# Seven-product projection: all sums on VectorE, and v units of four token blocks

## The chip, the cores and the metric

One core of a Trainium2 chip runs the whole program. The metric is device microseconds (us) of one execution; a profiled execution also gives its span, from the first to the last instruction. The engines are TensorE (PE; PEld is its weight load), VectorE (DVE), ScalarE (ACT), GpSimd (POOL) and SyncE (SP), whose queue issues most DMAs.

## What is computed

A two-layer trunk on 2048 prompt frames and 64 further frames (2112 columns, T), width 1024, four heads:

```
for each layer i:                       # 0: differential attention, 1: stick-breaking attention
    h = rmsnorm(x, norm_w[i])
    q, k, v, g = split(h @ w_in[i], 4)  # 1024 x 4096
    x = x + (mixer_i(q, k, v, past) * silu(g)) @ w_out[i]
y = rmsnorm(x, final_norm_w)            # returned with the new k and v rows of both layers
```

All matrices are fp32. A matmul is made of three: each operand is split into hi (a rounded copy, by ACT) and lo (the rest, x - hi, by DVE or POOL), and lo*hi, hi*lo and hi*hi are summed in PSUM.

## The kernel before, in words

Layer 0 runs `p_phase` (projection), `a_phase` (attention) and `o_phase` (output); layer 1 runs `p_strassen`, `a_phase` and `o_phase`. The change lies in layer 1's projection, `p_strassen` (L349), in `stage_steps` (L318), which prepares its input and runs inside layer 0's `o_phase` and inside `p_strassen`, and in the few lines that hand the norm's factors over.

`p_strassen` multiplies 2x2 block matrices with seven products in place of eight. The tokens come in two passes: pass 0 has two blocks of 512 tokens, pass 1 two blocks of 512 + 32. Seven operands of the token side (sums of blocks) lie in DRAM (`xop`); `fill` (L379) loads each in four chunks through three buffers `xraw` (pool `sf`, 3 buffers), and each chunk is split by ACT (L53) and by `split`'s second engine (L54). The seven operands X stand in SBUF for the whole pass, and are refilled for pass 1 product by product during the last unit of pass 0 (L573).

The work is a list of units (L513 to L518). Pass 0: head 0's k, q, gate; four v units; for heads 1 to 3 gate, k, q. Pass 1: four heads' k and q; v, v, s, v, v, s; four gates. A "p" unit (k, q or gate of one head) has seven products of 12 matmuls with 512 columns (pass 0) or 24 with 272 columns (pass 1). A v unit holds two token blocks of 128, seven products of 24 matmuls with 256 columns, one block to a PSUM bank. An s unit is the 64 left-over tokens' v, classically.

For each unit `seven` (L400) loads four weight quarters (two sets for v), forms four sums (L406, L407, L409 on POOL, L411), and `halves` (L387) splits seven operands `wop` (14 for v; ACT L53, then L54). `wop` has five buffers; `more`/`take` (L523, L528) run that far ahead of the products. `other()` (L375) gives the lo of each split in turn to POOL and to DVE.

A unit's seven products go to four PSUM tags of two banks each: a, e, c, d, and again a, c, d, accumulated onto what stands there. Between them ACT copies a or c out (L579, L584, L592) and DVE adds a product to an SBUF tile `e` (L581, L587, L596, L599; ten buffers); L588 is on POOL. Four times a unit `finish` (L439) stores a result: for q, k and v a split into `s` and DMAs, for a gate a silu of L457 ACT, L458 DVE, L459 and L460 ACT, L461 POOL, L462 and L463 DVE. PE may start product 5 only when L579 has read bank a, and product 7 only when L587 has read bank d.

`stage_steps` for pass 1 runs one step after each of units 3 to 6 (the v units of pass 0), L606: eight loads, eight scalings (L334, four of them of 32 columns), four sums (L337, L338; L342 and L343 on POOL), four small stores and seven stores. Unit 7 frees its tiles and loads `xs`.

The order of instructions within each engine's queue is set at build time, by a scheduler that goes by priorities and its own estimate of times, not strictly by program order; each queue then runs in order.

Of the kernel before, what the change touches and what calls it, by code (L numbers as in the profile page):

```python
# [17 lines left out]
P = 128  # L18
# [3 lines left out]
NS = 64  # L22
# [33 lines left out]

def mm3(nc, ps, lh, ll, rh, rl, start, stop):
    nc.tensor.matmul(ps, lh, rl, start=start, stop=False, skip_group_check=True)  # L58
    nc.tensor.matmul(ps, ll, rh, start=False, stop=False, skip_group_check=True)  # L59
    nc.tensor.matmul(ps, lh, rh, start=False, stop=stop, skip_group_check=True)  # L60
# [257 lines left out]
def stage_steps(nc, k, pas, xv, rr, alloc):  # L318

    w, sides = PASSES[pas]
    dst = k.xop[pas]
    for c in range(4):
        b = {}
        for d in range(2):
            for t in range(2):
                b[d, t] = q = alloc()[:, :w]
                for p0, t0, n in sides[t]:  # L330
                    nc.sync.dma_start(out=q[:, p0:p0 + n], in_=xv[:, c + 4 * d, t0:t0 + n])
        for (d, t), q in b.items():
            for (p0, t0, n), r in zip(sides[t], rr[t]):
                nc.vector.scalar_tensor_tensor(q[:, p0:p0 + n], q[:, p0:p0 + n], k.wnm[:, c + 4 * d:c + 4 * d + 1],  # L334
                                               r, ALU.mult, ALU.mult)
# [6 lines left out]
        nc.gpsimd.tensor_tensor(b[0, 1], b[1, 1], b[0, 1], ALU.subtract)  # L342
        nc.gpsimd.tensor_tensor(t4, b[1, 0], t2, ALU.subtract)  # L343
        for i, q in enumerate((b[0, 0], t2, t1, b[0, 1], b[1, 0], b[1, 1], t4)):
            nc.sync.dma_start(out=dst[i, :, c, :w], in_=q)
        yield


def p_strassen(tc, k, layer, xsrc, rb, close):  # L349
# [7 lines left out]
    with ExitStack() as es:  # L357
# [8 lines left out]
        xv = xsrc.rearrange("(c p) t -> p c t", p=P)  # L366
        turn = [0]

# [5 lines left out]

        def other():  # L375
            turn[0] += 1
            return nc.gpsimd if turn[0] % 2 else nc.vector

        def fill(pas, op):  # L379
            w = PASSES[pas][0]  # L380
            X[op] = t = xp.tile([P, 2, 4, PW], F32R, tag=f"x{op}", name="x")
            for c in range(4):
                raw = rp.tile([P, PW], F32, tag="r", name="xraw")[:, :w]
                nc.sync.dma_start(out=raw, in_=k.xop[pas][op, :, c, :w])
                split(nc, t[:, 0, c, :w], t[:, 1, c, :w], raw, other())

        def halves(a):  # L387
            t = wop.tile([P, 2, 512], F32R, tag="w", name="wop")
            split(nc, t[:, 0], t[:, 1], a, other())
            return t  # L390
# [9 lines left out]
        def seven(a11, a12, a21, a22):  # L400

            a11, a21, a22 = raws((a11, a21, a22))
            s1 = wrp.tile([P, 512], F32, tag="w", name="s1")
            s2 = wrp.tile([P, 512], F32, tag="w", name="s2")
            a12, = raws((a12,))
            nc.vector.tensor_tensor(s1, a21, a22, ALU.add)  # L406
            nc.vector.tensor_tensor(s2, s1, a11, ALU.subtract)  # L407
            yield halves(a11)
            nc.gpsimd.tensor_tensor(a21, a11, a21, ALU.subtract)  # L409
            yield halves(s2)  # L410
            nc.vector.tensor_tensor(s2, a12, s2, ALU.subtract)  # L411
# [26 lines left out]

        def finish(u, o, fh, th):  # L439

            w = PASSES[u.pas][0]
            if u.kind == "v":
                hs = slice((u.i + 2 * fh) * HW, (u.i + 2 * fh + 1) * HW)
                t0 = PASSES[u.pas][1][th][0][1] + u.b * 256
# [3 lines left out]
                split(nc, s2[:, 0, :512], s2[:, 1, :512], o[:, :512], other())  # L448
                for i in range(2):
# [5 lines left out]
            if u.s == 3:  # L455
# [13 lines left out]
            s2 = sp.tile([P, 2, PW], F32R, tag="s2", name="s2")  # L469
            split(nc, s2[:, 0, :w], s2[:, 1, :w], o, other())  # L470
            store(lambda t0, n: dst[r0:r0 + P, :, t0:t0 + n], lambda p0, n: s2[:, :, p0:p0 + n].bitcast(F32), th, u.pas)

        def product(u, ps, ws, x, start):
            if u.kind == "v":
                for b in range(2):
                    t = slice((2 * u.b + b) * P, (2 * u.b + b + 1) * P)
                    for c in range(4):
                        ce = slice(c % 2 * HW, c % 2 * HW + HW)
                        mm3(nc, ps[:, b, :HW], x[:, 0, c, t], x[:, 1, c, t], ws[c // 2][:, 0, ce],
                            ws[c // 2][:, 1, ce], start and c == 0, c == 3)  # L480
                return
# [9 lines left out]
        def unit(pas, kind, **kw):  # L491
# [3 lines left out]
            u.__dict__.update(kw)  # L495
            u.n, u.subs = (HW, 2) if kind == "v" else ((512, 1), (272, 2))[pas]
            u.tiles = 1 if kind == "p" else 2
# [59 lines left out]
        for n, u in enumerate(units):  # L557
# [5 lines left out]

            def view(t):
                return t[:, :u.subs * u.n].rearrange("p (b n) -> p b n", b=u.subs)

            def run(op, tag, start):
# [5 lines left out]
                if refill:  # L573
                    fill(1, op)
                return ps[tag][:, :u.subs, :u.n]

            a = run(0, "a", True)
            m = e()
            nc.scalar.activation(view(m), a, AF.Copy)  # L579
            b = run(1, "e", True)  # L580
            nc.vector.tensor_tensor(view(m), view(m), b, ALU.add)  # L581
            c = run(2, "c", True)
            m5 = e()
            nc.scalar.activation(view(m5), c, AF.Copy)  # L584
            d = run(3, "d", True)
            x = e()
            nc.vector.tensor_tensor(view(x), view(m), d, ALU.add)  # L587
            nc.gpsimd.tensor_tensor(view(m5), view(x), view(m5), ALU.add)  # L588
            finish(u, m5, 1, 1)
            a = run(4, "a", False)  # L590
            o = e()
            nc.scalar.activation(view(o), a, AF.Copy)  # L592
            finish(u, o, 0, 0)
            c = run(5, "c", False)
            o = e()
            nc.vector.tensor_tensor(view(o), view(m), c, ALU.add)  # L596
            finish(u, o, 0, 1)
            d = run(6, "d", False)
            nc.vector.tensor_tensor(view(m), view(m), d, ALU.add)  # L599
            finish(u, m, 1, 0)  # L600
            if n == 0:
                stats(nc, k, k.acc, TT[0][1], lambda: bank("a")[:, 0], rb[:, 832:1088], None, e(), e())
                staging = stage_steps(nc, k, 1, xv, ((rb[:, :512], rb[:, 1024:1056]), (rb[:, 512:1024], rb[:, 1056:1088])), e)
            elif n >= 3 and staging is not None:
                if next(staging, 0) == 0:
                    staging = None  # L606
                    close()
                    xs = es.enter_context(pool(tc, f"sv{layer}", side="right")).tile([P, 2, NC, NS], F32R, name="xs")
                    raw = e()[:, :NC * NS].rearrange("p (c t) -> p c t", c=NC)
                    nc.sync.dma_start(out=raw, in_=k.xs)  # L610
                    split(nc, xs[:, 0], xs[:, 1], raw, nc.vector)

# [360 lines left out]
def o_phase(tc, k, layer, resid, rb):  # L973
# [3 lines left out]
    with ExitStack() as es:  # L977
# [39 lines left out]
        for n, ti in enumerate((1, 2, 3, 4, 0) if last else (1, 3, 2, 4, 0)):  # L1017
# [196 lines left out]
```

## Time and profile before

| | us |
|---|---|
| median of 3 runs (3048.54 to 3050.07) | 3049.37 |
| the profiled execution, own time | 3052.32 |
| its span | 3050.3 |
| of that, `p_strassen` (1528 to 2318) | 790 |
| mean granted TensorE clock over the span | 0.97 |

The profile's rows come from the one profiled execution. "Busy" is the time in which an engine has an instruction running; an instruction that stands and waits for something inside itself is busy too. Matmuls overlap one another, so a PE busy all the time is not yet PE at its best. A wait names the instruction that ended it.

### The profile page before, as it was taken

How to read it: one execution, taken by the hardware profiler on the slowest of the kernel's cores; microseconds unless marked ns; L12 is line 12 of the kernel's file. 1: busy time of each engine (PE TensorE's matmuls, PEld its weight loads, DVE VectorE, ACT ScalarE, POOL GpSimd, SP SyncE). 2: the span in 40 equal slices, each digit the busy share in tenths (PEclk: the TensorE clock that was granted, in tenths of full speed). 3: DMA queues.
4: the chain of work that ended last, by engine and by line, in shares of the span. 5: the costliest groups of instructions: out<-in, count | busy, mean ns of one | idle time of the engine just before them, and what ended most of it. 6: DMA issues, size and time to landing. Idle time of an engine off the chain costs nothing. (4 is left out here: it accounts for less than half of the span.)

```text
span 3050.3 us, 46001 instructions
## 1 busy us (share of the span) xinstructions
PE 2850.7 (93%) x16342; PEld 2473.8 (81%) x16342; DVE 2010.3 (66%) x3266; ACT 1420.8 (47%) x2706; POOL 1175.2 (39%) x1053
## 2 busy tenths in 40 slices
PE   8899999999899999999977899799897999999998
PEld 7888998989777777778857777699796778888788
DVE  8754625245688777854558877655886878878454
ACT  5321221212566665643244344444455777776433
POOL 4533333333144343551256755645763000000221
PEclk9999999999999999999988999999997999999999
DMA  5476556463633425155756844655746344433442
GB/s 164 152 204 180 143 156 171 144 162 113 231 133 130 141 95 181 63 169 185 243 183 217 274 145 148 219 191 190 228 131 207 117 150 137 134 125 101 159 148 95
DMA packets 370550, 492.43 MB, mean 161 GB/s; under 512 B 64016, under 2 KB 208656, under 8 KB 370320
## 3 DMA queue, kind: packets, MB, share of 16 engines
q1 hardware_dynamic: 355168, 475.06, 49.0%
q10 hardware_dynamic: 15152, 14.44, 1.4%
q8 instruction: 128, 2.10, 0.3%
q14 instruction: 102, 0.84, 0.1%
HBM read 281.49 MB, written 207.88 MB: 160 GB/s over the span
## 5 line engine op out<-in xcount | busy, mean ns | idle before, releaser
L58 PE MATMUL pj<-x,wop 128*128 128x272 f32 (+1 forms) x1008 | 336.8, 335 | 48.0 <-POOL x L54 19.2
L58 PE MATMUL pj<-hl,whi 128*128 128x512 f32 (+2 forms) x960 | 341.0, 355 | 2.6 <-ACT whi L53 1.9
L59 PE MATMUL pj<-hh,wlo 128*128 128x512 f32 (+2 forms) x960 | 338.8, 353 | 0.1
L60 PE MATMUL pj<-hh,whi 128*128 128x512 f32 (+2 forms) x960 | 338.4, 353 | 0.0
L59 PE MATMUL pj<-x,wop 128*128 128x272 f32 (+1 forms) x1008 | 332.5, 330 | 0.1
L60 PE MATMUL pj<-x,wop 128*128 128x272 f32 (+1 forms) x1008 | 331.8, 330 | 0.0
L58 PE MATMUL s<-k,q 128*128 128x512 f32 (+3 forms) x656 | 268.6, 410 | 33.7 <-POOL k L54 13.5
L58 PE MATMUL o<-wl,v 128*128 128x512 f32 (+4 forms) x688 | 270.1, 393 | 17.4 <-DVE wl L54 9.9
L58 PEld LDWEIGHTS pj<-x,wop 128*128 128x128 f32 x1008 | 193.6, 192 | 80.0 <-POOL x L54 24.0
L54 DVE TENSOR_TENSOR wl<-tp,wh 128x512 fp32r<-128x512 f32 (+5 forms) x344 | 195.2, 575 | 93.3 <-ACT wh L53 92.9
L60 PE MATMUL o<-wh,v 128*128 128x512 f32 (+4 forms) x688 | 249.8, 363 | 0.0
L59 PE MATMUL o<-wh,v 128*128 128x512 f32 (+4 forms) x688 | 249.5, 363 | 0.0
L60 PE MATMUL s<-k,q 128*128 128x512 f32 (+3 forms) x656 | 245.2, 374 | 0.0
L59 PE MATMUL s<-k,q 128*128 128x512 f32 (+3 forms) x656 | 244.8, 373 | 0.0
L53 ACT ACTIVATE s<-o 128x256 fp32r<-128x256 f32 (+2 forms) x212 | 84.1, 404 | 337.9 <-DMA kS<-s 127.4
L58 PE MATMUL ps<-ol,wh 128*128 128x512 f32 (+2 forms) x640 | 227.8, 356 | 6.4 <-DVE ol L54 6.4
L53 ACT ACTIVATE wh<-tp 128x512 fp32r<-128x512 f32 (+5 forms) x344 | 170.8, 508 | 131.1 <-PE tp L776 115.2
L59 PE MATMUL ps<-oh,wl 128*128 128x512 f32 (+2 forms) x640 | 229.6, 359 | 0.0
L60 PE MATMUL ps<-oh,wh 128*128 128x512 f32 (+2 forms) x640 | 227.0, 355 | 0.0
L59 PEld LDWEIGHTS pj<-x,wop 128*128 128x128 f32 x1008 | 194.7, 193 | 15.0 <-DVE wop L54 0.6
L60 PEld LDWEIGHTS pj<-x,wop 128*128 128x128 f32 x1008 | 194.0, 193 | 15.6
L58 PEld LDWEIGHTS pj<-hl,whi 128*128 128x128 f32 x960 | 182.0, 190 | 26.5 <-ACT whi L53 2.1
(231 smaller groups left out, 7887.7 us busy)
## 6 DMA issues: line engine op xcount, KB each, us to landing
wraw<-in_wqkg SPq DMA_DIRECT2D x144, 256.0 KB, 3.9
vS<-s SPq DMA_DIRECT2D x128, 256.0 KB, 3.2
v<-vS SPq DMA_DIRECT2D x64, 512.0 KB, 5.3
q<-qS SPq DMA_DIRECT2D x60, 512.0 KB, 5.2
k<-kS SPq DMA_DIRECT2D x60, 512.0 KB, 7.8
wraw<-in_wv SPq DMA_DIRECT2D x96, 256.0 KB, 3.8
qS<-s SPq DMA_DIRECT2D x128, 128.0 KB, 2.4
kS<-s SPq DMA_DIRECT2D x128, 128.0 KB, 2.4
```

The source lines that it names most:

```text
L53: nc.scalar.activation(hi, x, AF.Copy)
L54: lo_eng.tensor_tensor(lo, x, hi.bitcast(F32), ALU.subtract)
L58: nc.tensor.matmul(ps, lh, rl, start=start, stop=False, skip_group_check=True)
L59: nc.tensor.matmul(ps, ll, rh, start=False, stop=False, skip_group_check=True)
L60: nc.tensor.matmul(ps, lh, rh, start=False, stop=stop, skip_group_check=True)
```

## The change

Within `p_strassen` and `stage_steps` every sum that POOL made goes to DVE: `other()` is gone and all lo parts are DVE's, as are L409, L461, L588, L342 and L343. A v unit takes four token blocks, two to a PSUM bank (the second block's first matmul has no start flag and is pinned behind the first block's matmuls), so there are two v units for four in each pass, and each weight operand is made once for four blocks; each PSUM bank is read by an instruction of its own, into an `e` tile of its own. The stage's steps for pass 1 go from behind units 3 to 6 to behind units 6, 7, 9 and 10 of the new numbering (head 1's k and q, head 2's k and q), its end to behind unit 11 (head 3's gate). The norm's factors lie as 2 x 544 columns, so one scaling of 544 columns takes the place of one of 512 and one of 32; three ACT copies put the left-over columns in place after unit 0.

```
 def mm3(nc, ps, lh, ll, rh, rl, start, stop, pin=None):
+    first = nc.tensor.matmul(ps, lh, rl, ...)
+    if pin is not None: pin(first)
 ...
 # stage_steps
-            for (p0, t0, n), r in zip(sides[t], rr[t]):
-                nc.vector.scalar_tensor_tensor(q[:, p0:p0 + n], ...)
+            nc.vector.scalar_tensor_tensor(q, q, k.wnm[...], rr[t], ALU.mult, ALU.mult)
-        nc.gpsimd.tensor_tensor(b[0, 1], ...)     # and t4
+        nc.vector.tensor_tensor(b[0, 1], ...)     # and t4
 ...
 # fill, halves, finish
-                split(..., other())
+                split(..., nc.vector)
 # seven, finish (gate)
-            nc.gpsimd.tensor_tensor(a21, a11, a21, ALU.subtract)
+            nc.vector.tensor_tensor(a21, a11, a21, ALU.subtract)
-                nc.gpsimd.tensor_tensor(a, a, r, ALU.mult)
+                nc.vector.tensor_tensor(a, a, r, ALU.mult)
 ...
 # product, v
-                for b in range(2):
-                    t = slice((2 * u.b + b) * P, (2 * u.b + b + 1) * P)
+                for b in range(4):
+                    t = slice(b * P, b * P + P)
+                    o = ps[:, b // 2, b % 2 * HW:b % 2 * HW + HW]
                     for c in range(4):
-                        mm3(nc, ps[:, b, :HW], ..., start and c == 0, c == 3)
+                        mm3(nc, o, ..., start and c == 0 and b % 2 == 0, c == 3,
+                            tc.keep_in_program_order if start and c == 0 and b % 2 else None)
 # values
-                for b in range(2):
-                    unit(pas, "v", i=i, b=b)
+                unit(pas, "v", i=i)
 ...
 # a unit: two pieces for v, one for the others
+            if u.kind == "v":
+                cut = [(lambda t, i=i: t[:, i], lambda t: t[:, :512]) for i in range(2)]
-            m = e()
-            nc.scalar.activation(view(m), a, AF.Copy)
+            m = [e() for _ in cut]
+            for (b, v), t in zip(cut, m):
+                nc.scalar.activation(v(t), b(a), AF.Copy)
 ...                                               # likewise for e, c, d, a, c, d
-            nc.gpsimd.tensor_tensor(view(m5), view(x), view(m5), ALU.add)
+                nc.vector.tensor_tensor(v(t5), v(tx), v(t5), ALU.add)
 ...
             if n == 0:
+                r = e()[:, :256]
+                stats(nc, k, k.acc, ..., r, None, e(), e())
+                for c0, c1, r0 in ((0, 192, 864), (192, 224, 512), (224, 256, 1056)):
+                    nc.scalar.activation(rb[:, r0:r0 + c1 - c0], r[:, c0:c1], AF.Copy)
+                staging = stage_steps(nc, k, 1, xv, (rb[:, :PW], rb[:, PW:]), e)
-            elif n >= 3 and staging is not None:
+            elif n in (6, 7, 9, 10):
+                next(staging)
+            elif n == 11:
+                next(staging, None)
+                close()
 ...
```

## Rows read from the trace of the kernel before

**Rows 1.** The page's part 1: busy time, share of the span and number of instructions of each engine.
```profile
PE 2850.7 (93%) x16342; PEld 2473.8 (81%) x16342; DVE 2010.3 (66%) x3266; ACT 1420.8 (47%) x2706; POOL 1175.2 (39%) x1053
```
**Rows 2.** Busy time by stage: layer 1's input side (the end of layer 0's `o_phase`) and `p_strassen`. Columns: stretch, its length, then busy us (and instructions) of each engine, granted clock, DMA share, GB/s.
```profile
1345.00:1528.00 183.00, 176.77 (x925) 153.86 (x923) 96.91 (x137) 51.55 (x97) 45.47 (x36) 0.99 0.66 220
1528.00:2318.00 790.00, 705.39 (x4466) 636.75 (x4466) 557.81 (x598) 362.90 (x640) 493.37 (x328) 0.95 0.58 187
```
**Rows 3.** The same columns for stretches cut at the first matmul of a unit (84 matmuls make a p unit of pass 0, 168 one of pass 1 or a v unit): head 0's k and q; its gate; the four v units; head 1's gate to head 3's k (8 units); head 3's q, and head 0's k and q of pass 1; the next six k and q units; v, v, s, v, v, s; the four gates. Then two single units, pass 1's first v and head 2's k in pass 0, and last a part of the fourth v unit.
```profile
1530.20:1590.80 60.60, 50.27 (x171) 35.54 (x172) 30.08 (x37) 29.14 (x51) 36.13 (x26) 0.85 0.57 182
1590.80:1610.30 19.50, 19.50 (x86) 15.75 (x85) 12.63 (x16) 10.06 (x18) 10.39 (x9) 1.00 0.54 176
1610.30:1729.30 119.00, 95.41 (x674) 92.93 (x673) 106.71 (x114) 51.55 (x90) 86.44 (x55) 0.89 0.78 251
1729.30:1903.40 174.10, 161.57 (x675) 127.04 (x673) 123.35 (x142) 74.52 (x135) 101.33 (x68) 0.97 0.48 161
1903.40:1990.50 87.10, 70.56 (x421) 62.93 (x420) 55.63 (x52) 41.08 (x73) 58.95 (x40) 0.92 0.67 215
1990.50:2117.10 126.60, 126.60 (x1011) 126.60 (x1010) 67.88 (x79) 49.73 (x85) 61.40 (x45) 1.00 0.58 188
2117.10:2228.80 111.70, 95.71 (x770) 91.43 (x769) 87.21 (x84) 60.33 (x107) 85.48 (x55) 1.00 0.74 235
2228.80:2316.80 88.00, 85.75 (x674) 84.50 (x672) 72.41 (x77) 43.64 (x79) 51.25 (x33) 1.00 0.24 75
2117.10:2137.10 20.00, 20.00 (x171) 20.00 (x170) 13.09 (x15) 11.87 (x20) 14.47 (x10) 1.00 0.64 204
1816.30:1844.50 28.20, 22.68 (x85) 17.30 (x84) 22.06 (x23) 13.42 (x25) 18.58 (x12) 0.89 0.31 101
1705.15:1731.30 26.15, 23.38 (x154) 22.49 (x155) 26.07 (x26) 10.97 (x20) 20.94 (x13) 0.87 0.88 290
```
**Rows 4.** PE's waits from 1528 to 2318: who waited for whom, us in total, times, longest.
```profile
PE pj L58 <- DVE wop L54: 26.0, 12, 4.5
PE pj L58 <- POOL x L54: 19.2, 10, 5.9
PE pj L58 <- DVE e L587: 12.3, 7, 4.2
```
**Rows 5.** DVE in order of time, around the last v unit of pass 0: start, us, what.
```profile
1699.64 0.68 DVE L406 TENSOR_TENSOR s<-wraw 128x512 f32<-128x512 f32 x1
1700.24 0.68 DVE L411 TENSOR_TENSOR s<-wraw,s 128x512 f32<-128x512 f32 x1
1700.84 0.67 DVE L599 TENSOR_TENSOR e<-e,pj 128x512 f32<-128x512 f32 x1
...
1711.85 0.71 DVE L337 TENSOR_TENSOR e<-e 128x544 f32<-128x544 f32 x1
1712.49 1.27 DVE L334 SCALAR_TENSOR_TENSOR e<-e,wnm,rb 128x32 f32<-128x32 f32 x1
```
**Rows 6.** POOL in order of time, the same stretch.
```profile
1718.76 1.72 POOL L409 TENSOR_TENSOR wraw<-wraw 128x512 f32<-128x512 f32 x1
1720.45 1.73 POOL L588 TENSOR_TENSOR e<-e 128x512 f32<-128x512 f32 x1
```
**Rows 7.** The instructions of single lines from 1528 to 2318: count, ns min/median/max, first and last start.
```profile
L458 DVE TENSOR_SCALAR e<-e x30: 409/443/1528, 1606.2 to 2319.2; 128x512 f32<-128x512 f32 x16, 128x544 f32<-128x544 f32 x14
L54 DVE TENSOR_TENSOR x<-xraw,x x28: 677/796/1881, 1529.3 to 1973.5; 128x512 fp32r<-128x512 f32 x14, 128x544 fp32r<-128x544 f32 x14
L54 POOL TENSOR_TENSOR x<-xraw,x x28: 1263/1351/1856, 1528.9 to 1975.6; 128x512 fp32r<-128x512 f32 x14, 128x544 fp32r<-128x544 f32 x14
```
**Rows 8.** One chunk's round in the refill, in order of time: SP's issue of the load, ACT's hi, POOL's lo.
```profile
1952.18 2.23 SPq L384 DMA_DIRECT2D xraw<-xop  x3
1954.92 0.66 ACT L53 ACTIVATE x<-xraw 128x544 fp32r<-128x544 f32 x1 [1.74 <-DMA xraw<-xop]
1955.65 1.34 POOL L54 TENSOR_TENSOR x<-xraw,x 128x544 fp32r<-128x544 f32 x1 [2.17 <-ACT x L53]
```
**Rows 9.** Waits of ACT and POOL from 1528 to 2318, as in rows 4.
```profile
POOL wop L54 <- ACT wop L53: 68.9, 42, 4.9
POOL e L461 <- ACT e L460: 51.2, 23, 3.3
POOL s L54 <- ACT s L53: 45.7, 31, 4.0
POOL x L54 <- ACT x L53: 44.7, 17, 12.2
ACT x L53 <- DMA xraw<-xop: 41.9, 29, 5.2
```
**Rows 10.** DVE in order of time in head 2's k unit, behind head 2's gate.
```profile
1834.58 0.68 DVE L462 SCALAR_TENSOR_TENSOR e<-e 128x512 f32<-128x512 f32 x1
1835.18 1.75 DVE L407 TENSOR_TENSOR s<-s,wraw 128x512 f32<-128x512 f32 x1
1836.85 1.75 DVE L463 SCALAR_TENSOR_TENSOR e<-e 128x512 f32<-128x512 f32 x1
1838.52 0.67 DVE L587 TENSOR_TENSOR e<-e,pj 128x512 f32<-128x512 f32 x1
```
**Rows 11.** DMA issues from 1528 to 2318: count, KB each, median us to landing.
```profile
wraw<-in_wv SPq DMA_DIRECT2D x80, 256.0 KB, 3.9
```

More of the change, by code (lines that the diff above doesn't have):

```diff
@@ L54, in split, with mm3 @@
     lo_eng.tensor_tensor(lo, x, hi.bitcast(F32), ALU.subtract)
-def mm3(nc, ps, lh, ll, rh, rl, start, stop):
-    nc.tensor.matmul(ps, lh, rl, start=start, stop=False, skip_group_check=True)
+def mm3(nc, ps, lh, ll, rh, rl, start, stop, pin=None):
+    first = nc.tensor.matmul(ps, lh, rl, start=start, stop=False, skip_group_check=True)
+    if pin is not None:
+        pin(first)
     nc.tensor.matmul(ps, ll, rh, start=False, stop=False, skip_group_check=True)
@@ L332, in stage_steps @@
         for (d, t), q in b.items():
[L333 to L335 removed]
+            nc.vector.scalar_tensor_tensor(q, q, k.wnm[:, c + 4 * d:c + 4 * d + 1], rr[t], ALU.mult, ALU.mult)
         t1, t2, t4 = alloc()[:, :w], alloc()[:, :w], alloc()[:, :w]
@@ L341, in stage_steps @@
                 nc.sync.dma_start(out=k.xs[:, c + 4 * d, 32 * t:32 * t + 32], in_=q[:, 512:544])
-        nc.gpsimd.tensor_tensor(b[0, 1], b[1, 1], b[0, 1], ALU.subtract)
-        nc.gpsimd.tensor_tensor(t4, b[1, 0], t2, ALU.subtract)
+        nc.vector.tensor_tensor(b[0, 1], b[1, 1], b[0, 1], ALU.subtract)
+        nc.vector.tensor_tensor(t4, b[1, 0], t2, ALU.subtract)
         for i, q in enumerate((b[0, 0], t2, t1, b[0, 1], b[1, 0], b[1, 1], t4)):
@@ L366, in p_strassen @@
         xv = xsrc.rearrange("(c p) t -> p c t", p=P)
-        turn = [0]
         def e():
@@ L373, in bank @@
             return psp.tile([P, 2, 512], F32, tag=tag, name="pj")
-        def other():
-            turn[0] += 1
-            return nc.gpsimd if turn[0] % 2 else nc.vector
         def fill(pas, op):
@@ L384, in fill @@
                 nc.sync.dma_start(out=raw, in_=k.xop[pas][op, :, c, :w])
-                split(nc, t[:, 0, c, :w], t[:, 1, c, :w], raw, other())
+                split(nc, t[:, 0, c, :w], t[:, 1, c, :w], raw, nc.vector)
         def halves(a):
             t = wop.tile([P, 2, 512], F32R, tag="w", name="wop")
-            split(nc, t[:, 0], t[:, 1], a, other())
+            split(nc, t[:, 0], t[:, 1], a, nc.vector)
             return t
@@ L437, in store, with finish @@
                 nc.sync.dma_start(out=dst(t0, n), in_=o(p0, n))
-        def finish(u, o, fh, th):
+        def finish(u, o, fh, th, half=0):
             w = PASSES[u.pas][0]
@@ L443, in finish @@
                 hs = slice((u.i + 2 * fh) * HW, (u.i + 2 * fh + 1) * HW)
-                t0 = PASSES[u.pas][1][th][0][1] + u.b * 256
+                t0 = PASSES[u.pas][1][th][0][1] + half * 256
                 nc.sync.dma_start(out=k.v[layer, t0:t0 + 256, hs].rearrange("(b p) e -> p b e", p=P),
@@ L447, in finish @@
                 s2 = sp.tile([P, 2, PW], F32R, tag="s2", name="s2")
-                split(nc, s2[:, 0, :512], s2[:, 1, :512], o[:, :512], other())
+                split(nc, s2[:, 0, :512], s2[:, 1, :512], o[:, :512], nc.vector)
                 for i in range(2):
@@ L469, in finish @@
             s2 = sp.tile([P, 2, PW], F32R, tag="s2", name="s2")
-            split(nc, s2[:, 0, :w], s2[:, 1, :w], o, other())
+            split(nc, s2[:, 0, :w], s2[:, 1, :w], o, nc.vector)
             store(lambda t0, n: dst[r0:r0 + P, :, t0:t0 + n], lambda p0, n: s2[:, :, p0:p0 + n].bitcast(F32), th, u.pas)
@@ L474, in product @@
             if u.kind == "v":
-                for b in range(2):
-                    t = slice((2 * u.b + b) * P, (2 * u.b + b + 1) * P)
+                for b in range(4):
+                    t = slice(b * P, b * P + P)
+                    o = ps[:, b // 2, b % 2 * HW:b % 2 * HW + HW]
                     for c in range(4):
                         ce = slice(c % 2 * HW, c % 2 * HW + HW)
-                        mm3(nc, ps[:, b, :HW], x[:, 0, c, t], x[:, 1, c, t], ws[c // 2][:, 0, ce],
-                            ws[c // 2][:, 1, ce], start and c == 0, c == 3)
+                        mm3(nc, o, x[:, 0, c, t], x[:, 1, c, t], ws[c // 2][:, 0, ce],
+                            ws[c // 2][:, 1, ce], start and c == 0 and b % 2 == 0, c == 3,
+                            tc.keep_in_program_order if start and c == 0 and b % 2 else None)
                 return
@@ L495, in unit @@
             u.__dict__.update(kw)
-            u.n, u.subs = (HW, 2) if kind == "v" else ((512, 1), (272, 2))[pas]
+            u.n, u.subs = (512, 2) if kind == "v" else ((512, 1), (272, 2))[pas]
             u.tiles = 1 if kind == "p" else 2
@@ L562, in p_strassen @@
             ps = {}
-            def view(t):
-                return t[:, :u.subs * u.n].rearrange("p (b n) -> p b n", b=u.subs)
+            if u.kind == "v":
+                cut = [(lambda t, i=i: t[:, i], lambda t: t[:, :512]) for i in range(2)]
+            else:
+                cut = [(lambda t: t[:, :u.subs, :u.n],
+                        lambda t: t[:, :u.subs * u.n].rearrange("p (b n) -> p b n", b=u.subs))]
             def run(op, tag, start):
@@ L574, in run @@
                     fill(1, op)
-                return ps[tag][:, :u.subs, :u.n]
+                return ps[tag]
             a = run(0, "a", True)
-            m = e()
-            nc.scalar.activation(view(m), a, AF.Copy)
-            b = run(1, "e", True)
-            nc.vector.tensor_tensor(view(m), view(m), b, ALU.add)
+            m = [e() for _ in cut]
+            for (b, v), t in zip(cut, m):
+                nc.scalar.activation(v(t), b(a), AF.Copy)
+            f = run(1, "e", True)
@@ L582, in p_strassen @@
+            for (b, v), t in zip(cut, m):
+                nc.vector.tensor_tensor(v(t), v(t), b(f), ALU.add)
             c = run(2, "c", True)
-            m5 = e()
-            nc.scalar.activation(view(m5), c, AF.Copy)
+            m5 = [e() for _ in cut]
+            for (b, v), t in zip(cut, m5):
+                nc.scalar.activation(v(t), b(c), AF.Copy)
             d = run(3, "d", True)
-            x = e()
-            nc.vector.tensor_tensor(view(x), view(m), d, ALU.add)
-            nc.gpsimd.tensor_tensor(view(m5), view(x), view(m5), ALU.add)
@@ L589, in p_strassen @@
-            finish(u, m5, 1, 1)
+            x = [e() for _ in cut]
+            for (b, v), t, tx, t5 in zip(cut, m, x, m5):
+                nc.vector.tensor_tensor(v(tx), v(t), b(d), ALU.add)
+            for i, ((b, v), tx, t5) in enumerate(zip(cut, x, m5)):
+                nc.vector.tensor_tensor(v(t5), v(tx), v(t5), ALU.add)
+                finish(u, t5, 1, 1, i)
             a = run(4, "a", False)
-            o = e()
-            nc.scalar.activation(view(o), a, AF.Copy)
-            finish(u, o, 0, 0)
+            for i, (b, v) in enumerate(cut):
+                o = e()
+                nc.scalar.activation(v(o), b(a), AF.Copy)
+                finish(u, o, 0, 0, i)
@@ L594, in p_strassen @@
             c = run(5, "c", False)
-            o = e()
-            nc.vector.tensor_tensor(view(o), view(m), c, ALU.add)
-            finish(u, o, 0, 1)
+            for i, ((b, v), t) in enumerate(zip(cut, m)):
+                o = e()
+                nc.vector.tensor_tensor(v(o), v(t), b(c), ALU.add)
+                finish(u, o, 0, 1, i)
             d = run(6, "d", False)
-            nc.vector.tensor_tensor(view(m), view(m), d, ALU.add)
-            finish(u, m, 1, 0)
+            for i, ((b, v), t) in enumerate(zip(cut, m)):
+                nc.vector.tensor_tensor(v(t), v(t), b(d), ALU.add)
+                finish(u, t, 1, 0, i)
@@ L601, in p_strassen @@
             if n == 0:
-                stats(nc, k, k.acc, TT[0][1], lambda: bank("a")[:, 0], rb[:, 832:1088], None, e(), e())
-                staging = stage_steps(nc, k, 1, xv, ((rb[:, :512], rb[:, 1024:1056]), (rb[:, 512:1024], rb[:, 1056:1088])), e)
-            elif n >= 3 and staging is not None:
[L605 to L611, printed above, removed]
+                r = e()[:, :256]
@@ new lines, in p_strassen @@
+                stats(nc, k, k.acc, TT[0][1], lambda: bank("a")[:, 0], r, None, e(), e())
+                for c0, c1, r0 in ((0, 192, 864), (192, 224, 512), (224, 256, 1056)):
[6 more added lines that the diff above has]
+                close()
+                xs = es.enter_context(pool(tc, f"sv{layer}", side="right")).tile([P, 2, NC, NS], F32R, name="xs")
+                raw = e()[:, :NC * NS].rearrange("p (c t) -> p c t", c=NC)
+                nc.sync.dma_start(out=raw, in_=k.xs)
+                split(nc, xs[:, 0], xs[:, 1], raw, nc.vector)
@@ L993, in o_phase @@
             ra = es.enter_context(pool(tc, f"ora{layer}")).tile([P, 1024], F32, name="ra")
-            rt = {1: ra[:, :512], 3: ra[:, 512:], 2: rb[:, :512], 4: rb[:, 512:832]}
+            rt = {1: ra[:, :512], 3: ra[:, 512:], 2: rb[:, :512], 4: rb[:, PW:PW + 320]}
         psp = es.enter_context(pool(tc, f"ops{layer}", 6, space=PSUM))
@@ L1060, in o_phase @@
             if ti == 3 and not last:
-                staging = stage_steps(nc, k, 0, yo, ((rt[1],), (rt[3],)),
+                staging = stage_steps(nc, k, 0, yo, (rt[1], rt[3]),
                                       lambda: stp.tile([P, 512], F32, tag="st", name="st"))
```

## Prediction

> **What bounds the kernel now.** I read the page's part 1 first [rows 1]: PE is busy 93% of the span, DVE 66%, POOL 39%. On that alone a change of DVE and POOL would be worth nothing. But the share is a mean over stages, so next comes the busy time by stage [rows 2]. Of `p_strassen`'s 790 us PE is busy 705 (85 idle), its clock is below full (0.95), and POOL is busier (493) than anywhere else. PE's waits in that stage name who ends the idle time [rows 4]: the lo parts of the weights, of the token operands X, and L587, DVE's read of bank d. PE waits for DVE and POOL, not for memory.
>
> The stage has to be cut by unit, since its parts have different limits [rows 3]. Some stretches have a PE that never stops, and these give a floor for each kind of unit: a p unit of pass 0 takes 19.5 us (the first gate), a v unit of two blocks 20.0, a p unit of pass 1 126.6 / 6 = 21.1. The s units' 96 small matmuls at 21.1 / 168 = 0.126 us come to 12. Time above the floor, stretch by stretch:
>
> 1. head 0's k and q: 60.6, floor 39.0, 21.6 above
> 2. its gate: 19.5, none
> 3. four v units: 119.0, floor 80.0, 39.0 above
> 4. eight units to head 3's k: 174.1, floor 156.0, 18.1 above
> 5. refill of X: 87.1, floor 19.5 + 42.2 = 61.7, 25.4 above
> 6. six k and q units: 126.6, none
> 7. v, v, s, twice: 111.7, floor 92.0, 19.7 above
> 8. four gates: 88.0, floor 84.4, 3.6 above
>
> Together 786.6 us, 127.4 above the floor. That is all this change can win, and it includes what the lowered clock costs, since the floors are at the full clock of 2.4 GHz. In stretch 3 the clock is 0.89 because PE stops again and again.
>
> **What a sum costs.** Here duration and price differ. Alone, a DVE sum of 512 columns lasts 0.68 us, but the next one starts 0.60 after it [rows 5]: 0.60 is its price in a full queue, and a PSUM read, which lasts the same, gets it too. For 544 columns it is 0.64, from 1711.85 to 1712.49. L458 lasts 0.41, or 0.33 by the same overlap of 0.08 [rows 7]. POOL needs 1.26 at best for the same sum [rows 7]. When both have work, DVE sums last up to 1.88 [rows 7] and POOL's start 1.69 apart [rows 6]. Two engines with full queues then finish one sum each in about 1.7 us, where DVE alone would do two in 1.20. So the move takes work from POOL and gives DVE back the time that it stood beside POOL.
>
> A rule speaks against it. The Trainium skill (Perfetto Trace Analysis, Optimizing Scalar/DVE Operations) says that with a saturated DVE it may make sense to hand work to ScalarE or even GpSimd, though it adds that GpSimd shares a read port with DVE and this might not help. By its first half the gates (stretch 8) would grow by POOL's 33 sums there at 0.60, 19.8 us, and the gain below would be 68 in place of 87; the rows just read [rows 5, 6] agree with its second half.
>
> **The change, part by part.** DVE's new load by unit:
> - k or q of pass 0: 7 lo parts of weights, 4 sums of `seven`, L588, 4 lo parts of results, 4 PSUM reads, 20 x 0.60 = 12.0 us. Pass 1: 11 x 0.60 + 9 x 0.64 = 12.4.
> - gate: 16 x 0.60 + 4 x (0.33 + 3 x 0.60) = 18.1; pass 1 the same with 544 columns, 18.9.
> - v of four blocks: 14 lo, 8 sums, 8 PSUM reads, 2 times L588, 8 lo, 40 x 0.60 = 24.0 against 40 us of PE. A v unit of two blocks had 31 sums for 20 us of PE; merging takes away 14 lo parts, 8 sums and 8 loads for each pair. Over both passes that is 56 splits on ACT as well, 32 of the 80 loads of `in_wv` [rows 11].
> - a step of staging: 4 scalings and 4 sums of 544, 8 x 0.64 = 5.1; the four scalings of 32 columns go.
> - fills: 28 x 0.60 = 16.8, refill 28 x 0.64 = 17.9. An s unit 5.5.
>
> Sums by stretch against the floor: (1) 40.8 of 39.0; (2) 18.1 of 19.5; (3) 48.0 of 80.0; (4) 3 x 18.1 + 5 x 12.0 + 4 x 5.1 = 134.7 of 156; (5) 54.7 of 61.7; (6) 74.4 of 126.6; (7) 59.0 of 92.0; (8) 75.6 of 84.4. DVE has 505.6 us to do, with POOL gone, where it was busy 557.8 beside POOL's 493.4 [rows 2]. No stretch but the first asks for more than PE's floor.
>
> What stands beside DVE in two stretches is the chunk's round. Three `xraw` buffers turn over in 2.74 (issue to ACT's start), 0.73 (to the lo's start), 1.34 of lo and 0.03 to the next issue [rows 8], 4.84 us. With DVE's lo at 0.72 it is 4.2, so a chunk comes every 1.4 us and an operand of four every 5.6. In the refill the seventh is ready 2.8 + 7 x 5.6 = 42 us after head 3's q begins, and PE wants it at 19.5 + 18 = 37.5: some 5 are lost at least, I take 10 with DVE's queue in between. ACT's waits for these loads [rows 9] shrink and don't go. In stretch 1 the 28 chunks come to 39 us at that pace.
>
> Forecast by stretch: (1) 49; (2) 20; (3) 83; (4) 165, the nine us above the floor for steps that now meet gates; (5) 72; (6) 126.6; (7) 95.5; (8) 88, unchanged, since DVE's 0.90 of PE leaves no room. Sum 699.1, a gain of 87.5.
>
> Bounds. (1) 41 to 60.6; (2) 19.5 to 24; (3) 80 to 100; (4) 156 to 182 (three gates at what head 2's cost its k unit, 28.2 - 19.5 = 8.7 each [rows 3]); (5) 66 to 84; (7) 92 to 104; (8) 84.4 to 96. Together 666 to 777: gains of 121 to 10.
>
> Edits costed at nothing: the move of L342 and L343 in layer 0's `o_phase`, 8 sums or 5 us of a DVE that is busy 97 of 183 there, beside a PE at 177 [rows 2]. The three ACT copies after unit 0 (under 0.66 each [rows 8]), on an engine busy 29 of 60. Two blocks to a bank and the pin: PE keeps all its matmuls, and nothing in the trace shows a second block in a bank. I bound that by zero and by one evacuation of 0.60 for each of 28 v products, 17 us, and take zero, since pass 1's p units fill two banks at the floor. The moved steps take 8 loads and 11 stores each on SP's queue, away from the v units' stores (24 each now) to those of k, q and gates; between the last step's stores and the refill that reads them now lies one unit, 19.5 us, for a landing of some 3.9 [rows 11]. Without that cover the refill starts later, at up to 4 us. The `xs` load moves too, with twelve units to spare.
>
> A wait is moved as well: whatever POOL waited for, DVE now waits for, with everything behind it. Queued behind are PSUM reads, L587 above all, for which PE waits with product 7.
>
> The profiled execution took 3052.32 us, 2.95 over the median. Less 87.5 it would take 2964.8, and the median 3049.4 - 87.5 = 2962.
>
> **Rivals.**
> - Gates hold up L587. L462, L407 and L463 stood ahead of it [rows 10], and head 2's k lost 8.7. The order in the queue stays the builder's; if every gate of pass 0 costs 8.7 and those of pass 1 half, (2) is 28.2, (4) 182.1, (8) 101.8, the gain 48, the time 3001. For: steps now share the ten `e` tiles with gates. Against: of the 1.75 us sums in that row none would last over 0.7. 0.24.
> - DVE is saturated where it is over 0.85 of PE's floor, in (4) and (8): POOL's sums there (68 and 33) come on top of the time before at 0.60 each, (4) 214.9, (8) 107.8, the gain 17.8, the time 3032. Against: in (8) DVE was busy 72.4 beside POOL and has 75.6 to do without it. 0.05. This is where the first half of that rule of the Trainium skill (Perfetto Trace Analysis, Optimizing Scalar/DVE Operations) would lead.
> - Slower: waits pile up in one queue. DVE was idle 232 of 790 us, and POOL waited 210.5 for ACT [rows 9]. If a share y of these 442.7 stays, now all on DVE, the stage takes 505.6 + 442.7 y, and from y = 0.635 on it is slower. At 0.75 it is 837.6, the time 3100. For: each lo follows its hi, on another engine. Against: those are mostly waits of engines that had run ahead, and in the worst stretch DVE was busy 26.07 of 26.15 us [rows 3]. 0.09; near y = 0.635 nothing changes, 0.03.
> - PE at its floor nearly everywhere: 666, the time 2928. DVE's load would allow it, the chunk's round and the scheduler hardly. 0.06.
>
> **How the numbers follow.** The forecast's own case has 0.53, from 2938 to 2985. Faster by over 0.2% (6 us, about what a measurement of this kernel can tell) has 0.53 + 0.24 + 0.05 + 0.06 = 0.88, the same 0.03, slower 0.09. The range goes from 2938 to 3018: it takes in the gates' case and leaves out the floor, saturation, no change and slower for the most part, some 0.2.
>
> **What would show it.** POOL nearly empty in the stage; DVE's lo parts at 0.68 as their mean; v units of 40 to 42 us at full clock; the refill above its floor by 5 to 15 with ACT still waiting for `xraw`; PE's waits for `wop` nearly gone, those for L587 the longest left. It is wrong if DVE is busy over 600 us, if PE waits for DVE more than 60, or if the v units stay above 46 each.

## The result and the profile after

The changed kernel takes 2954.78 us (median of 4 runs, 2951.99 to 2956.65) against 3049.72 before in the same series: ratio 0.9686, 95% interval 0.967 to 0.9703. The forecast was 2962, in a range from 2938 to 3018. The profiled execution took 2956.65 us, its span is 2954.1.

Part 1 of the page [rows 1 before]. POOL's busy time almost halves; DVE's falls although it takes 240 more instructions.
```profile
PE 2821.3 (96%) x16342; PEld 2456.4 (83%) x16342; DVE 1966.7 (67%) x3506; ACT 1393.7 (47%) x2653; POOL 657.3 (22%) x709
```
The stretches of [rows 3], cut again at the first matmul of the same units (start; head 0's gate; v; heads 1 to 3; refill; k and q; v and s; gates). Columns as there: PE, PEld, DVE, ACT, POOL, clock, DMA share, GB/s.
```profile
1528.60:1587.00 58.40, 48.24 (x171) 33.38 (x172) 42.06 (x67) 31.72 (x58) 0.00 (x0) 0.92 0.65 208
1587.00:1606.50 19.50, 19.50 (x86) 15.75 (x85) 13.66 (x22) 9.97 (x17) 0.00 (x0) 1.00 0.34 119
1606.50:1686.40 79.90, 79.90 (x674) 79.90 (x673) 53.71 (x87) 34.25 (x60) 0.00 (x0) 1.00 0.58 189
1686.40:1844.70 158.30, 156.46 (x674) 125.85 (x673) 139.59 (x229) 77.79 (x139) 0.00 (x0) 1.00 0.73 245
1844.70:1920.00 75.30, 66.98 (x421) 61.36 (x420) 56.80 (x90) 39.58 (x70) 0.00 (x0) 0.93 0.74 244
1920.00:2046.90 126.90, 126.90 (x1011) 126.90 (x1010) 82.82 (x123) 51.26 (x87) 0.00 (x0) 1.00 0.59 193
2046.90:2140.90 94.00, 92.32 (x770) 91.06 (x769) 58.08 (x93) 42.33 (x77) 0.00 (x0) 1.00 0.69 218
2140.90:2226.10 85.20, 84.73 (x674) 84.29 (x672) 70.78 (x117) 48.45 (x85) 0.13 (x2) 1.00 0.29 93
```
The v units stand at PE's floor and at the full clock, where the clock was 0.89. The start is nearly as slow as before. PE's waits in the stage [rows 4], and the lo parts of the raw weight quarters on DVE, before and after (count, ns min/median/max):
```profile
PE pj L58 <- DVE x L54: 20.9, 18, 5.4
PE pj L58 <- ACT e L581: 1.8, 2, 1.3
PE pj L58 <- DVE wop L54: 1.4, 3, 0.6
```
```profile
L54 DVE TENSOR_TENSOR wop<-wraw,wop x88: 675/1135/1862, 1550.3 to 2308.9; 128x512 fp32r<-128x512 f32 x88
L54 DVE TENSOR_TENSOR wop<-wraw,wop x141: 676/685/694, 1540.5 to 2212.1; 128x512 fp32r<-128x512 f32 x141
```
Waits for weights are nearly gone (1.4 us), those for X are left. No lo part of a weight lasts over 0.694 us now; the longest lo part of the stage, one of 544 columns, lasts 0.728.

One gain lies behind the stage. PE's gap between the last product and attention's first matmul was 12.78 us and is 6.22. Both times POOL's lo of k ends just before that matmul; the experiments show what it had stood behind. Before, then after:
```profile
2329.56 0.53 PE L58 MATMUL s<-k,q 128*64 128x320 f32 x1 [12.78 <-POOL k L54]
```
```profile
2225.86 0.29 PE L62 MATMUL pj<-x,wop 128*128 128x272 f32 x1
2232.36 0.53 PE L58 MATMUL s<-k,q 128*64 128x320 f32 x1 [6.22 <-DMA gT<-e]
```

### The profile page after: what moved, and what is told of

It is laid out like the page before. It is cut to its first block, busy times and chain, and to the rows that moved or that the text cites. A ratio compares the mean times of both kernels' runs of the same rounds, so it can differ in the third digit from the quotient of the medians.

```text
span 2954.1 us, 45378 instructions
## 1 busy us (share of the span) xinstructions
PE 2821.3 (96%) x16342; PEld 2456.4 (83%) x16342; DVE 1966.7 (67%) x3506; ACT 1393.7 (47%) x2653; POOL 657.3 (22%) x709
## 4 chain that ended last, share of the span: by engine, by line
PE 69%; DVE 16%; DMA 6%; ACT 6%; issue 3%; POOL 0%; SPq 0%; DVEq 0%; ACTq 0%; POOLq 0%
PE pj L58 14%; PE pj L61 14%; PE pj L62 14%; DVE rowA L773 4%; PE ps L58 3%; PE ps L61 3%; PE ps L62 3%; PE o L58 3%; PE o L61 3%; PE o L62 3%; PE tp L789 2%; DVE rowA L770 2%; PE s L58 2%; PE s L62 2%; PE s L61 2%
## 5 line engine op out<-in xcount | busy, mean ns | idle before, releaser
L58 PE MATMUL pj<-x,wop 128*128 128x272 f32 (+1 forms) x1008 | 329.6, 329 | 26.0 <-DVE x L54 20.9
L61 PE MATMUL pj<-x,wop 128*128 128x272 f32 (+1 forms) x1008 | 328.7, 326 | 0.0
L62 PE MATMUL pj<-x,wop 128*128 128x272 f32 (+1 forms) x1008 | 327.9, 327 | 0.0
L754 POOL MEMSET z<- 128x1 f32 (+1 forms) x68 | 11.8, 174 | 1149.4 <-PE pj L62 775.4
L58 PEld LDWEIGHTS pj<-x,wop 128*128 128x128 f32 x1008 | 191.4, 190 | 51.1 <-DVE x L54 24.8
L61 PEld LDWEIGHTS pj<-x,wop 128*128 128x128 f32 x1008 | 192.1, 191 | 14.9 <-DVE wop L54 0.7
L62 PEld LDWEIGHTS pj<-x,wop 128*128 128x128 f32 x1008 | 191.4, 190 | 15.1
```

What stands on the lines that cost most here:

```text
L58: first = nc.tensor.matmul(ps, lh, rl, start=start, stop=False, skip_group_check=True)
L754: nc.gpsimd.memset(z[:nq, nk:nk + 1], 0.0)
```

## The experiments

Ten kernels ran, each in three rounds against the kernel before, which took 3053 to 3056 us there. Times of different series are therefore compared by their ratios; 0.001 is 3 us. Stretch lengths are from the one profile of each kernel, worked out from the first matmul of each unit; "gap" is the one before attention.

| us | start | v | heads 1-3 | refill | v, s | gates | gap | ratio (95%) |
|---|---|---|---|---|---|---|---|---|
| before | 60.6 | 119.0 | 174.1 | 87.1 | 111.7 | 88.0 | 12.8 | 1 |
| after | 58.4 | 79.9 | 158.3 | 75.3 | 94.0 | 85.2 | 6.2 | 0.9686 (0.967-0.9703) |
| dve_only | 59.0 | 103.3 | 162.4 | 73.9 | 100.3 | 86.0 | 6.2 | 0.9785 (0.9765-0.9806) |
| four_pool | 61.9 | 80.1 | 183.6 | 81.5 | 102.5 | 87.6 | 12.8 | 0.9851 (0.9829-0.9873) |
| dve_two_moved | 57.8 | 84.0 | 162.3 | 74.5 | 101.4 | 86.0 | 6.3 | 0.9726 (0.971-0.9742) |
| staging_early | 58.0 | 79.9 | 167.3 | 73.5 | 95.7 | 85.2 | 6.2 | 0.9708 (0.9686-0.973) |
| gates_pool | 57.9 | 79.9 | 159.8 | 74.3 | 95.3 | 88.1 | 12.7 | 0.9723 (0.9708-0.9737) |
| gate_sum_pool | 58.5 | 79.9 | 160.7 | 73.5 | 94.9 | 85.2 | 10.0 | 0.9693 (0.9677-0.9709) |
| e9 | 58.2 | 79.9 | 161.7 | 72.8 | 94.8 | 85.1 | 6.2 | 0.9688 (0.9671-0.9705) |
| xraw4 | 48.9 | 79.9 | 163.7 | 70.9 | 95.2 | 85.2 | 6.2 | 0.9654 (0.9633-0.9676) |
| x4w11 | 49.6 | 79.9 | 157.4 | 65.9 | 101.0 | 84.4 | 6.8 | 0.9637 (0.9623-0.9651) |
| x4acc | 49.0 | 79.9 | 162.1 | 70.9 | 94.2 | 84.9 | 6.3 | 0.9643 (0.9629-0.9657) |

How far a single profile can be trusted is seen in gate_sum_pool: up to the last four gates its instructions stand in the same order as the whole change's in every queue of the stage, with the same tiles, and yet heads 1 to 3 differ by 2.4 us and the refill by 1.8. Differences of that size in these two columns show nothing.

**The parts of the change.** dve_only is the kernel before with

```
-            return nc.gpsimd if turn[0] % 2 else nc.vector
+            return nc.vector
-            nc.gpsimd.tensor_tensor(...)   # L342, L343, L409, L461, L588
+            nc.vector.tensor_tensor(...)
```

> The kernel before with every POOL sum of the seven-product projection moved to VectorE and nothing else: v units stay at two blocks, staging stays behind them. Theory (a sum costs DVE 0.60 us once POOL is gone, where a POOL and a DVE sum together took 1.7): a v unit asks DVE for 31 x 0.60 + 5.1 of staging = 23.7 us against PE's 20, so stretch 3 comes to 96 to 100 (119 before, 79.9 with the whole change); heads 1 to 3 (no staging there) 157; refill 75; the last v and s units 98 to 102; the gates 85. In all 70 us under before, about 2978. Rival 1 (the merging of v units does it, the engine does not matter): within 10 us of before, 3040 to 3050. Rival 2 (the engine is all of it): 2955, as with the whole change.

The ratio is 0.9785: 63.6 us under the kernel before of its series, where 70 were expected. Neither rival holds; the engine alone is worth about two thirds of the whole gain. The v stretch came to 103.3, above the 96 to 100, and heads 1 to 3 to 162.4 in place of 157. With staging behind every v unit PE waits 13.6 us for `wop` there, and DVE is busy 93 of 103:
```profile
1611.30:1714.50 103.20, 88.36 (x673) 85.48 (x672) 93.08 (x162) 49.43 (x86) 0.00 (x0) 0.95 0.88 284
```
```profile
PE pj L58 <- DVE wop L54: 13.6, 9, 4.6
```

four_pool is the whole change with `other()`, L404, L456, L594, L342 and L343 back on POOL.

> The whole change with POOL put back where it was (every second lo part, L404, L456, L594 and two sums of staging): four-block v units and moved staging alone. Theory: forty sums of a v unit shared at 1.7 us a pair are 34 us against PE's 40, so stretch 3 falls to 82 to 88; but staging now meets gates with POOL slow, so head 1 to 3 grow from 174 to 185 or 190; refill and start stay at 87 and 60; the PE gap before attention stays at 12 to 13. In all 25 to 40 under before, 3010 to 3025. Rival 1 (merging is all of it): 2955 to 2970. Rival 2 (the engine is all of it): 3040 to 3050.

The ratio is 0.9851, 3010.2 us, at the fast end of what the theory gave; the refill fell to 81.5 in place of staying at 87. The v units are at the floor with POOL too (80.1), and heads 1 to 3 are worse than before (183.6). There PE's longest wait is for DVE's read of bank d (L598 in this kernel), the case that the prediction had as its likeliest rival: 11.6 of the 17.3 us that PE stands idle in that stretch.
```profile
PE pj L58 <- DVE e L598: 11.6, 6, 4.3
PE pj L58 <- ACT e L587: 2.1, 4, 1.1
```
Ahead of L598 in DVE's queue stand sums of gates, of weights and of staging, single ones of them at 1.75 us in place of 0.68. Before the longest of these waits (4.3):
```profile
1804.40 1.75 DVE L408 TENSOR_TENSOR s<-s,wraw 128x512 f32<-128x512 f32 x1
1806.08 1.75 DVE L464 SCALAR_TENSOR_TENSOR e<-e 128x512 f32<-128x512 f32 x1
1807.74 0.67 DVE L598 TENSOR_TENSOR e<-e,pj 128x512 f32<-128x512 f32 x1
```
With DVE alone PE never waits for that read. dve_two_moved is dve_only with the staging moved:

```
-            elif n >= 3 and staging is not None:
+            elif n in (8, 9, 11, 12, 13) and staging is not None:
```

> All sums on VectorE with v units of two blocks, and the staging steps behind the same k and q units as in the whole change: the change without its four-block units. Theory (a two-block v unit asks DVE for 31 x 0.60 = 18.6 of PE's 20.0 us): the v stretch at 80 to 88, the last v and s units at 100 as with VectorE alone, heads 1 to 3 158 to 162; 6 to 15 us over the changed kernel, 2962 to 2970. Rival (a two-block unit can't be fed at 93% of DVE, with staging or without): the v stretch 95 or more, 2975 to 2985.

The v stretch is 84.0 as expected; the time, 2970.7, is just over the expected 2970, and by ratio 12 us over the changed kernel, within the 6 to 15. Step by step, from before to dve_only the ratio falls by 0.0215, with the staging moved by another 0.0059, and by another 0.0040 to the whole change, which adds the four blocks to a unit and the single scaling of 544 columns. This is one order of the steps; the moved staging with POOL and two-block units was not run. Two-block units can be fed once staging is away (84.0 of 80), and four blocks bring the rest and the later v and s units (101.4 to 94.0). staging_early puts the steps back in the whole change:

```
-            elif n in (6, 7, 9, 10):
+            elif n in (3, 4, 5, 6):
-            elif n == 11:
+            elif n == 7:
```

> The whole change with the staging steps put back behind units 3 to 6 (now v, v, and head 1's gate and k). Theory: DVE has 16 us of room in each v unit (24 of 40), a step asks 5.1, so the move in itself is worth little: within 5 us of the changed kernel, 2952 to 2960. Rival (the ten e tiles bind: a v unit of four blocks uses ten, a step seven more): the second v unit and head 1's units lose 8 us or more, 2965 to 2985.

By ratio this is 7 us over the changed kernel, but the two intervals overlap, so only the profile tells the kernels apart. It speaks for the rival, except that the second v unit loses nothing. The v units take a step for nothing (79.9), but head 1's k takes 29.6 us in place of 19.5 where two steps meet head 1's gate, in a single wait of PE for L581, ACT's copy into an `e` tile, which itself waited for the end of a gate's chain (L458):
```profile
PE pj L58 <- ACT e L581: 8.5, 1, 8.5
```
```profile
1726.39 0.60 ACT L581 ACTIVATE e<-pj 128x512 f32<-128x512 f32 x1 [6.33 <-DVE e L458]
```

**POOL's help, tested on its own.** gates_pool gives POOL its sums back in the four gates of pass 1 only, gate_sum_pool only the one sum L456 there. In short:

```
 # gates_pool: every second lo part, L404, L456, L594
+            nc.gpsimd if u.pas == 1 and u.s == 3 else nc.vector
 # gate_sum_pool: L456
-                nc.vector.tensor_tensor(a, a, r, ALU.mult)
+                (nc.gpsimd if u.pas else nc.vector).tensor_tensor(a, a, r, ALU.mult)
```

> The whole change with all of POOL's sums given back in the four gates of pass 1 alone: every second lo part, L404, L456, L594. DVE's load is highest there. Theory: the pair of engines does no more than DVE alone, stretch 8 goes from 85.2 to 87 to 89 and the gap before attention from 6.2 to 12 to 13, 8 to 11 us over the changed kernel. Rival (a saturated DVE gains from handing work to POOL, the rule of the Trainium skill, Perfetto Trace Analysis, Optimizing Scalar/DVE Operations): stretch 8 at PE's floor of 84.4 to 85, and whatever the gap costs is all there is.

> The whole change with one sum given back to POOL, L456 of the four gates of pass 1 (16 of them). Theory: attention's first lo part of k is POOL's and stands in its queue behind the last gate's sums, so PE's gap between the last product and attention's first matmul goes from 6.2 to 10 to 13 us; the gates stay at 85 to 86; 4 to 8 us over the changed kernel. Rival (that gap is set by the release of tiles and by loads): the gap stays at 6 to 7 and the time within 2 us of the changed kernel.

gates_pool came out as its theory had it: the gates take 88.1 and the gap 12.7, 9.4 us together on the span's two parts, and by ratio it is 11 us slower than the changed kernel. DVE is busy longer with POOL's help than without (70.78), though it does 38 instructions fewer:
```profile
2145.60:2233.70 88.10, 85.74 (x675) 84.58 (x674) 76.05 (x79) 44.38 (x80) 52.67 (x33) 1.00 0.29 90
```
The rule's first half (the Trainium skill, Perfetto Trace Analysis, Optimizing Scalar/DVE Operations) does not hold here. DVE is not full in the gates, though, with 70.78 of 85.20 us. Nearer to the rule's own case are heads 1 to 3 of the changed kernel, with 139.59 of 158.30, and there four_pool, with POOL back, took 183.6.

The gap is the gates' tail, and it is not POOL's queue that makes it long here:
```profile
2242.99 1.87 POOL L467 TENSOR_TENSOR e<-e 128x544 f32<-128x544 f32 x1 [1.42 <-ACT e L466]
2243.59 1.57 DVE L464 TENSOR_SCALAR e<-e 128x544 f32<-128x544 f32 x1
2245.19 0.66 ACT L465 ACTIVATE e<-e 128x544 f32<-128x544 f32 x1 [1.73 <-DVE e L464]
2245.76 0.61 ACT L53 ACTIVATE k<-raw 128x512 fp32r<-128x512 f32 x1
2246.45 1.27 POOL L54 TENSOR_TENSOR k<-raw,k 128x512 fp32r<-128x512 f32 x1 [1.59 <-ACT k L53]
```
POOL stood idle for 1.59 us until ACT had made k's hi. That hi stood in ACT's queue behind a gate's L465, which had waited 1.73 us for DVE's L464, and L464 lasted 1.57 us beside POOL's gate sum, where the same instruction lasts 0.44 in the changed kernel. ACT's queue also issues the load of that k: 8.7 us behind the start of the last product's last matmul here (2242.35 and 2233.66), 0.2 us ahead of it in the changed kernel. In the kernel before, POOL was idle for 1.58 us in the same place.

gate_sum_pool shows the gap alone: 10.0, with the gates at 85.2. There the lo of k does stand behind a POOL sum, for 1.4 us. Its ratio (0.9693) can't be told from that of the whole change, so that the 3.8 us cost the run as much rests on the profile; the 4 to 8 us of its theory are not shown.

**The start and the refill.** xraw4 has four xraw buffers and nine e tiles, e9 the nine e tiles alone, x4w11 takes the room from `wraw`, x4acc from the sum `acc`. In short:

```
-        rp = es.enter_context(pool(tc, f"sf{layer}", 3))
+        rp = es.enter_context(pool(tc, f"sf{layer}", 4))   # xraw4, x4w11, x4acc
-        ep = es.enter_context(pool(tc, f"se{layer}", 10))
+        ep = es.enter_context(pool(tc, f"se{layer}", 9))   # xraw4, e9
-        wrp = es.enter_context(pool(tc, f"sr{layer}", 12))
+        wrp = es.enter_context(pool(tc, f"sr{layer}", 11)) # x4w11
-        rb = rp.tile([P, 1088], F32, name="rb")            # x4acc
-        k.acc = rp.tile([P, TT[0][1]], F32, name="acc")
+        rb = rp.tile([P, 1120], F32, name="rb")
+        k.acc = rb[:, 864:1120]
```

> The whole change with four xraw buffers in place of three, and nine e tiles in place of ten to make room. Theory (the chunk's round of 4.2 us over the buffers bounds the start and the refill): a chunk every 1.1 us in place of 1.4 to 1.7; head 0's k and q in pass 0 58.3 -> 50 to 53, refill stretch 75.3 -> 68 to 70, in all 9 to 14 us under the changed kernel, 2941 to 2946. Rival 1 (DVE's queue or the order on PE bounds them): within 3 us of the changed kernel. Rival 2 (the e tiles bind elsewhere): slower than the changed kernel, 2960 or more, with the loss in the v units or gates.

> The whole change with nine e tiles in place of ten and nothing else. Theory (the ten e tiles bind where a staging step meets a gate: ACT's copy L581 waits for a tile and PE for it): stretch 4 163 to 165 with PE waiting for L581, start 58 and refill 75 as with ten, in all 4 to 7 us over the changed kernel. Rival (the e tile had no part; xraw4's loss came from the fourth xraw buffer's loads): stretch 4 at 158.

> The whole change with four xraw buffers; the room comes from the weights' raw tiles, eleven in place of twelve, and e stays at ten. Theory (xraw4 won 9.5 us at the start by the chunk's round and 4.4 in the refill, and lost 5.4 in stretch 4 to the missing e tile alone): start 49, stretch 4 back at 158, refill 71, v units still 80; 13 to 15 us under the changed kernel, ratio to the kernel before 0.9635 to 0.965. Rival (a v unit needs all twelve raw tiles): the v stretches grow, 80 to 84 or more, and the gain is lost.

> The whole change with four xraw buffers, ten e tiles and twelve raw tiles: the room comes from the norm's sum, which moves into columns of rb that are free until unit 0's end. Theory (each buffer cut so far cost its own stretch: e stretch 4, raw tiles stretch 7): start 49 to 51, stretch 4 158, refill 66 to 71, the last v and s units 94 to 95; 14 to 20 us under the changed kernel, ratio to the kernel before 0.961 to 0.964. Rival (a faster refill only moves the loss to the next wait): stretch 4 or 7 above that by 5 or more, ratio 0.965.

The chunk's round does bound the start: with four buffers it is 9 us shorter in all three kernels. The refill is 70.9, 65.9 and 70.9 with four buffers and 72.8 to 75.3 with three; why x4w11 has the shortest is open. The chunks' hi, lo and loads at the start, the whole change and then x4acc (first and last start at the end of the times):
```profile
L53 ACT ACTIVATE x<-xraw x27: 612/632/634, 1527.7 to 1569.3; 128x512 fp32r<-128x512 f32 x27
L54 DVE TENSOR_TENSOR x<-xraw,x x28: 682/691/694, 1527.9 to 1570.3; 128x512 fp32r<-128x512 f32 x28
L379 SPq DMA_DIRECT2D xraw<-xop x25: 319/319/753, 1528.6 to 1565.1; - x25
DMA to landing us min/median/max: 2.4/2.9/5.4
```
```profile
L53 ACT ACTIVATE x<-xraw x28: 613/630/635, 1529.2 to 1564.6; 128x512 fp32r<-128x512 f32 x28
L54 DVE TENSOR_TENSOR x<-xraw,x x28: 678/684/695, 1529.8 to 1565.3; 128x512 fp32r<-128x512 f32 x28
L379 SPq DMA_DIRECT2D xraw<-xop x24: 319/320/977, 1530.5 to 1559.1; - x24
```
The whole change's start in two parts, columns as in [rows 3], and the landing of the five loads issued in the second part:
```profile
1528.60:1557.00 28.40, 22.70 (x73) 14.23 (x73) 20.90 (x33) 15.69 (x27) 0.00 (x0) 0.90 0.66 201
1557.00:1570.30 13.30, 9.39 (x30) 6.43 (x31) 8.09 (x15) 8.01 (x15) 0.00 (x0) 0.87 0.91 303
```
```profile
DMA to landing us min/median/max: 4.2/4.9/5.4
```
e9 came out as neither its theory nor its rival had it: no loss in its ratio (0.9688), and heads 1 to 3 at 161.7. They came also to 162.1 in x4acc with ten tiles and to 160.7 in gate_sum_pool, which changes nothing there. The order in the queues is not the reason, since in that stretch it is the same in e9, in gate_sum_pool and in the whole change; e9's order is the same in the whole stage. So my reading that one e tile cost xraw4 5.4 us is not shown: xraw4 and x4acc, nine tiles and ten, have one order there too and lie 1.6 us apart. x4w11's loss of 7 us in v and s with eleven raw tiles, where PE waits 6.4 for `wop`, was its rival's, but the gain was not lost. x4acc lies between its theory and its rival. x4w11 and x4acc both lie under the whole change, by intervals that do not overlap its own, and can't be told from each other; xraw4's interval overlaps that of the whole change.

## Why the prediction was right, and where not

- **The price of a sum.** 0.60 us start to start on DVE alone, against 1.7 for one sum on each engine: held. All of DVE's work was put at 505.6 us (the eight terms as printed add up to 505.3); it is busy 517.5, where a sum with nothing close behind it counts with its full 0.68. dve_only's gain and gates_pool's loss both fit it.
- **The stretches.** The sum of the eight was forecast at 699.1 and is 697.5. That it comes so near is luck, since larger misses cancel: the start took 9.4 us more and the refill 3.3 more (75.3 for 72), heads 1 to 3 took 6.7 less (158.3 for 165), v 3.1 less (79.9 for 83), the gates 2.8 less and the last v and s 1.5 less. Merging two units into one holds v at the floor, as worked out from 24 us of DVE to 40 of PE; but merging brings only the last 4 of v's 39 us when it comes last, behind the engine and the moved staging.
- **The term that was mis-sized is the start**, 49 forecast and 58.4 measured. The step "in stretch 1 the 28 chunks come to 39 us at that pace" had the right mechanism (three buffers turning over), and its pace held at first: the first 21 of the 25 reissued loads start 1.42 us apart, for 1.4. The last four come 2.0 apart, for the five loads issued from 1557.0 on took 4.2 to 5.4 us to land, where the median of all is 2.9. In that time the queues moved 303 GB/s, with k's stores and the next weights among it, and 201 before; that this traffic is the cause is likely and not tested. Nor did PE run far ahead meanwhile: when the last lo began at 1570.3 there were still 16.7 us of the 39 to do, where 49 leaves 10, for which the prediction has no working. x4acc's 14.3 us behind its last lo at 1565.3 is of the same kind.
- **The gap before attention was missing from the sum**, 6.6 us: the prediction went through the work of the stage and not through what the next stage's first instructions stand behind. With sums on POOL that was mainly ACT's queue, held up by the last gates.
- **The signs.** POOL is empty in the stage, the weights' lo parts last 0.69 as their mean, the v units 40 us, the refill is 13.6 above its floor. One sign failed: PE's longest waits are those for X, and for L587's read (L592 after) it does not wait at all.
- **The clock.** That it was 0.89 in the third stretch of [rows 3] because PE stops again and again is not shown by these rows alone: in the seventh PE is idle 16.0 of 111.7 us at 1.00.
- **The rivals.** Gates holding up L587: not in the changed kernel, but two thirds of PE's idle time in that stretch of four_pool is of this kind, so the case was real, and it is the engine's change that removed it. Piled-up waits: 505.6 + 442.7 y = 697.5 gives y = 0.43, well under 0.635. Saturation by the rule of the Trainium skill (Perfetto Trace Analysis, Optimizing Scalar/DVE Operations): gates_pool and four_pool speak against it. The `e` tiles named there are what staging_early shows; in the changed kernel PE waits 1.8 us for L581, which itself stood behind other work of ACT and waited for no tile.

## What to carry to other kernels

Price an instruction by the distance between starts in a full queue, alone and beside the other engine; if two engines in turn finish a pair later than one of them alone would, move the work, but only after checking each stretch's sum on the one engine against the floor of the engine that bounds it. Cut a stage by its units to find that floor, since some unit nearly always shows it. When one engine is relieved, follow the first instructions of the next stage back through every queue that they stand in. When a load is bound by its buffers, look at its latency at that moment, and not only at its median. And before reading a few microseconds in a profile, find two kernels whose order is the same and see how far they lie apart.

## What was not expected of the hardware

A DVE that was given help got busier: 76.05 us for 79 instructions with POOL at work, 70.78 for 117 without. That is 0.96 us each against 0.60, and gates_pool's gates took 2.9 us longer.
